# First loads in pieces beside products of ones, and pinned pairs of 64-row products, in a two-block transformer kernel

## The chip, the cores and the metric

The kernel runs on one core of one Trainium2 chip. The metric is the device time of one execution in microseconds (us), shown as the median of three runs.

## The reference

Two transformer blocks of different make run one after the other on x (512 tokens, 1024 channels); memories of 256 tokens are attended in each. Cut to what matters:

```python
def first_block(x, mem, ...):
    h = rmsnorm(x, norm_mix_g[l])
    proj = h @ w_in[l]                       # gates, conv, q, k, v of 8 heads
    y_conv = short_conv_mixer(cb, cc, cx, conv_w[l], w_conv_out[l])
    y_attn = diff_attention(q, k, v, rel_bias, lam, lam_init, subln_g[l]) @ w_attn_out[l]
    x = x + (sigmoid(gc) * y_conv + sigmoid(ga) * y_attn) @ w_mix_out[l]
    x = x + cross_attention(rmsnorm(x, norm_cross_g[l]), rmsnorm(mem, norm_mem_g[l]), ...)
    x = x + peer_ffn(rmsnorm(x, norm_ffn_g[l]), ...)      # product-key experts
    return rmsnorm(x, final_g)

def second_block(x, mem, ...):
    z = rms_norm(x, mix_norm_g[l]) @ w_in[l]
    y_nsa = nsa_mixer(...)                   # 8 heads of 64, two k/v groups
    y = concat([rms_norm(y_nsa, g_nsa), rms_norm(y_gmlp, g_gmlp), rms_norm(y_conv, g_conv)])
    x = x + y @ w_out[l]
    x = x + memory_cross_attention(x, mem, xattn_norm_g[l], ...)
    x = x + conv_ffn(x, ffn_norm_g[l], ...)
    return rms_norm(x, final_norm_g)
```

In `diff_attention` the two halves of a head, and in `nsa_mixer` two heads of different groups, have 64 channels each: their logits are products over 64 rows.

## The kernel before

The program is `mix1`, `cross`, `peer`, `mix2`, `cross` and `ffn` in sequence. Activations lie with channels on the partitions (x is a tile 128 x 8 x 512), a linear layer (`lin`, L99) sums eight blocks k of 128 channels into a bank of PSUM.

Every product is done in three (`mm3`, L83): an operand is split into hi, a cast by ScalarE, and lo, the rest, by a subtraction on VectorE (`split`, L69), and lo x hi, hi x hi and hi x lo are summed. In `lin` the first (L85, with xl) and second (L86) need w_hi, the third (L87) needs w_lo. `weights` (L73) loads w_raw on SP's queue (four buffers) and splits it: w_hi at L70, w_lo at L71 (three buffers each). The input x is scaled by a gain from the packed vectors `pk` and split by `scaled` (L109): xh on ScalarE (L111), xl on VectorE (L112). Since the normalisation's factor is one per token, the linears run on x without it; the squares of x are summed beside (`square`, sq_acc, L137 and L140), summed over channels by products with ones (`colsum`, L129), turned into rstd by small steps on VectorE (`rsqrt`, L158 to L165) and spread to all partitions by L172 (`bcast`), which ScalarE copies out as rbc (L175). What leaves the linear is multiplied with it.

`mm3s` (L89) issues the three products for two items at once: for a pair of halves A and B that lie on partitions 0 to 63 and 64 to 127, first both lo products (L93), then both hi (L95), then both last (L97). It is used in `rows` of mix1 (L311, 32 groups) and in the attention of mix2 (L1331, 32 groups), with 256, 384 or 512 columns.

Within an engine, instructions run in a fixed order. A scheduler sets it when the program is built: it goes through the program as written with a model of costs and fills an engine that would wait with what is ready, except where `keep_in_program_order` pins instructions to the order in which they are written. So an edit in one place can move rows in another. In mix2, the products of the out-projection (`out_part`, L1312, and `half_out`, L1319) serve as such fillers. At its end, eight outputs of twelve products are made from the attention's part (L1360ff); each is multiplied with rbc (ev, L1365) and added to x (L1366), and the second `cross` (L462) splits the new x, sums its squares and makes its q from the weights wq (named `ps` and `pl`), while kl and vl are splits of the keys and values read back from DRAM.

At the start `consts` (L56) loads the pack and an identity on ScalarE's queue, `body` (L1529) loads the weights of the first linear (w_in[8]) and the eight rows of x on SP's queue, and `mix1` (L184) runs two linears ahead (w_in[8], w_in[16]) before the column sum of the squares.

```python
first = pr.weights(I["w_in"][8], KT)                          # body, L1538
for k in range(KT):
    nc.sync.dma_start(out=x[:, k, :], in_=I["xT"][k * P:(k + 1) * P, :])
...
ahead = [self.lin(first, xh, xl), self.lin(w_in[16], xh, xl)] # mix1
```

## Time and profile before

| | |
|---|---|
| median of three runs | 2920.49 us (2919.88 to 2922.27) |
| profiled execution | 2924.64 us |
| its span | 2922.70 us |
| mean granted TensorE clock | 0.989 |
| TensorE busy | 2840.0 us (97%) |
| VectorE busy | 2165.6 us (74%) |
| ScalarE busy | 1234.7 us (42%) |

PE is TensorE's products and PEld its weight loads, DVE is VectorE, ACT ScalarE, POOL GpSimd, SP the engine whose queue issues most loads. In the timeline an instruction stands with its start and duration; neighbours on TensorE overlap, so the step from one start to the next is the cost of a product. What is in brackets is the time for which the engine was idle before, and what ended it. x8 means that eight records of the same kind follow each other.

### The profile page before, as it was taken

The page shows a single profiled execution, that of the slowest core. Times are in us where ns is not written, and L with a number is a line of the kernel's source. Part 1 is how long each engine was busy: PE and PEld are TensorE (multiplying, and loading weights), DVE is VectorE, ACT ScalarE, POOL GpSimd, SP SyncE. Part 2 cuts the span into 40 slices and gives each one's busy share as a digit, 9 for nine tenths or more (in the row PEclk, how much of TensorE's full clock was granted, in tenths as well). Part 3 has the DMA queues.
Part 4 walks back from the last instruction along what each step waited for, and adds up shares of the span by engine and source line. Part 5 has one row for each costly group of instructions (what it writes and reads, how often), then busy time and mean ns, then how long its engine had stood idle before and what let it go on. Part 6 is the DMA issues. An engine that isn't in the chain of part 4 may idle for free.

```text
span 2922.7 us, 40044 instructions
## 1 busy us (share of the span) xinstructions
PE 2840.0 (97%) x14683; PEld 2448.4 (84%) x14683; DVE 2165.6 (74%) x4333; ACT 1234.7 (42%) x2053; POOL 534.2 (18%) x318
## 2 busy tenths in 40 slices
PE   8999999999997899999999999999979999999998
PEld 7887888888887899999998989887857778888887
DVE  6636667566899889787787787777796768688844
ACT  3234445444333598533333333333423655433322
POOL 0000000000036201344454454431131000000000
PEclk9999999999998999999999999999989999999999
DMA  4343233542233365899999899986512004233333
GB/s 162 100 136 115 90 98 98 180 133 67 88 107 123 108 228 219 314 346 333 341 332 317 322 341 337 324 293 206 170 59 83 25 19 128 75 94 98 95 97 104
DMA packets 200496, 504.67 MB, mean 173 GB/s; under 512 B 17475, under 2 KB 88259, under 8 KB 198764
## 3 DMA queue, kind: packets, MB, share of 16 engines
q1 hardware_dynamic: 155516, 333.22, 35.2%
q0 software_dynamic: 36864, 134.23, 12.7%
q10 hardware_dynamic: 7920, 34.66, 3.0%
q8 instruction: 116, 1.90, 0.3%
q14 instruction: 80, 0.66, 0.1%
HBM read 461.46 MB, written 40.59 MB: 172 GB/s over the span
## 4 chain that ended last, share of the span: by engine, by line
PE 82%; DVE 12%; ACT 2%; DMA 2%; issue 1%; ACTq 0%; DVEq 0%
PE ps L603 14%; PE ps L85 13%; PE ps L87 13%; PE ps L86 13%; PE pl L85 2%; PE pl L86 2%; PE pl L87 2%; PE pt L87 2%; PE pt L86 2%; PE pt L85 2%; PE po L85 2%; PE po L87 1%; PE po L86 1%; DMA v_raw<-in_peer_v_dram 1%; DVE yc L1067 1%
## 5 line engine op out<-in xcount | busy, mean ns | idle before, releaser
L70 ACT CAST w_hi<-w_raw 128x1024 fp32r<-128x1024 f32 (+2 forms) x277 | 281.3, 1015 | 533.6 <-PE ps L86 411.9
L85 PE MATMUL ps<-xl,w_hi 128*128 128x512 f32 x1224 | 487.1, 398 | 12.1 <-DVE xl L112 8.2
L86 PE MATMUL ps<-xh,w_hi 128*128 128x512 f32 x1224 | 482.6, 394 | 0.0
L87 PE MATMUL ps<-xh,w_lo 128*128 128x512 f32 x1224 | 481.5, 394 | 0.2 <-DVE w_lo L71 0.2
L71 DVE TENSOR_TENSOR w_lo<-w_raw,w_hi 128x1024 fp32r<-128x1024 f32 (+2 forms) x263 | 309.1, 1176 | 98.7 <-ACT w_hi L70 93.8
L595 POOL TENSOR_TENSOR w_lo<-w_raw,w_hi 128x1024 fp32r<-128x1024 f32 x33 | 94.6, 2872 | 1063.3 <-PE pl L645 837.8
L85 PEld LDWEIGHTS ps<-xl,w_hi 128*128 128x128 f32 x1224 | 231.4, 189 | 60.8 <-DVE xl L112 8.4
L87 PEld LDWEIGHTS ps<-xh,w_lo 128*128 128x128 f32 x1224 | 231.1, 189 | 49.8 <-DVE w_lo L71 0.8
L86 PEld LDWEIGHTS ps<-xh,w_hi 128*128 128x128 f32 x1224 | 231.7, 189 | 47.6 <-issue 1.8
L860 POOL DMA_INDIRECT row<-in_peer_v_dram,eidx x128 | 196.8, 1538 | 254.5 <-DVE ya L879 204.3
L860 POOL DMA_INDIRECT row<-in_peer_u_dram,eidx x128 | 186.6, 1457 | 221.3 <-DVE dots L867 185.8
L603 PE MATMUL ps<-hfh,w_hi 128*128 128x384 f32 x1024 | 206.4, 343 | 3.3 <-ACT ring L609 1.6
L594 ACT CAST w_hi<-w_raw 128x1024 fp32r<-128x1024 f32 x128 | 134.9, 1054 | 171.7 <-PE ps L603 135.4
L603 PE MATMUL ps<-hfh,w_lo 128*128 128x384 f32 x1024 | 201.9, 338 | 3.0 <-POOL w_lo L595 3.0
L603 PE MATMUL ps<-hfl,w_hi 128*128 128x384 f32 x1024 | 201.7, 338 | 0.0
L603 PEld LDWEIGHTS ps<-hfh,w_hi 128*128 128x128 f32 x1024 | 182.8, 190 | 11.2 <-ACT w_hi L594 2.6
L603 PEld LDWEIGHTS ps<-hfh,w_lo 128*128 128x128 f32 x1024 | 179.8, 190 | 3.4 <-POOL w_lo L595 3.4
L603 PEld LDWEIGHTS ps<-hfl,w_hi 128*128 128x128 f32 x1024 | 181.7, 190 | 0.1
L595 DVE TENSOR_TENSOR w_lo<-w_raw,w_hi 128x1024 fp32r<-128x1024 f32 x95 | 116.0, 1222 | 85.8 <-ACT w_hi L594 63.4
L70 ACT CAST wh<-ring 128x384 fp32r<-128x384 f32 x103 | 52.9, 513 | 291.1 <-PE pm L86 249.7
L912 DVE TENSOR_TENSOR v_lo<-v_raw,v_hi 128x1024 fp32r<-128x1024 f32 x128 | 156.2, 1220 | 19.9 <-ACT v_hi L911 18.8
L879 DVE SCALAR_TENSOR_TENSOR ya<-row,coef,ya 128x1024 f32<-128x1024 f32 x127 | 162.8, 1282 | 0.6
(496 smaller groups left out, 6351.5 us busy)
## 6 DMA issues: line engine op xcount, KB each, us to landing
w_raw<-in_u_t_dram SPq DMA_DIRECT2D x128, 512.0 KB
v_raw<-in_peer_v_dram SPq DMA_DIRECT2D x128, 512.0 KB
w_raw<-in_w_in_dram SPq DMA_DIRECT2D x82, 512.0 KB
Gd<-gs ACTq DMA_DIRECT2D x12, 2048.0 KB
gg<-Gd SPq DMA_DIRECT2D x32, 768.0 KB
w_raw<-in_ffn_w_up_dram SPq DMA_DIRECT2D x44, 512.0 KB
w_raw<-in_ffn_w_down_dram SPq DMA_DIRECT2D x20, 512.0 KB
w_raw<-in_w_pq_dram SPq DMA_DIRECT2D x16, 512.0 KB
```

The lines of the kernel that those rows point to most:

```text
L70: self.nc.scalar.copy(out=hi, in_=src)
L71: (eng or self.nc.vector).tensor_tensor(out=lo, in0=src, in1=hi.bitcast(F32), op=ALU.subtract)
L85: mm(out, ah, bl, start=start, stop=False)
L86: mm(out, ah, bh, start=False, stop=False)
L87: mm(out, al, bh, start=False, stop=stop)
L594: i = nc.scalar.copy(out=hi, in_=raw)
L595: (nc.gpsimd if ahead else nc.vector).tensor_tensor(out=lo, in0=raw, in1=hi.bitcast(F32), op=ALU.subtract)
L603: i = nc.tensor.matmul(ps, w[:, k, :], h[:, k, :], start=p == k == 0, stop=(p, k) == (2, KT - 1))
L860: nc.gpsimd.indirect_dma_start(out=r, out_offset=None, in_=src, in_offset=bass.IndirectOffsetOnAxis(ap=eidx[:, s:s + 1], axis=0))
L879: i = nc.vector.scalar_tensor_tensor(out=ya, in0=r, scalar=coef[:, s:s + 1], in1=ya, op0=ALU.mult, op1=ALU.add)
L912: pin(tt(out=vl, in0=raw, in1=vh.bitcast(F32), op=ALU.subtract))
L1067: stt(out=o, in0=hp[:, f, k:k + S], scalar=self.col("conv_dw_w_2", 2 * k + f), in1=o, op0=ALU.mult, op1=ALU.add)
```

## The change

It has two parts.

The start: `consts` loads only the first eight columns of the pack at once, and issues nine 128x128 products of a tile of ones with itself into a bank that nobody reads. A new `first` loads the first weights in four pieces of two blocks k each, each ahead of the two rows of x that go with it, on SP's queue; the second row goes on ScalarE's queue, followed there by the rest of the pack and the identity (`consts_late`). `mix1` splits these weights piece by piece in its loop over k. One small instruction, g8, that reads the late part of the pack is pinned to its place.

The pairs: of the six products of a group in `mm3s` all but A's first are pinned to the order in which they are written.

```diff
--- before.py
+++ after.py
@@ -56,11 +56,33 @@
     def consts(self):
         nc, c = self.nc, self.const
         self.pk = c.tile([P, self.I["pack"].shape[1]], F32, name="pk")
-        nc.scalar.dma_start(out=self.pk, in_=self.I["pack"])
+        nc.scalar.dma_start(out=self.pk[:, :KT], in_=self.I["pack"][:, :KT])
         self.idt = c.tile([P, P], F32, name="idt")
-        nc.scalar.dma_start(out=self.idt, in_=self.I["idt"])
         self.ones = c.tile([P, P], F32, name="ones")
         nc.vector.memset(self.ones, 1.0)
+
+        ps = self.misc.tile([P, S], F32, name="pm")
+        for _ in range(9):
+            nc.tensor.matmul(ps[:, :P], self.ones, self.ones, start=True, stop=True)
+
+    def consts_late(self):
+        self.nc.scalar.dma_start(out=self.pk[:, KT:], in_=self.I["pack"][:, KT:])
+        self.nc.scalar.dma_start(out=self.idt, in_=self.I["idt"])
+
+    def first(self, w, x, src):
+
+        nc, wp = self.nc, self.wp
+        raw = wp.tile([P, KT, P], F32, name="w_raw", bufs=4)
+        hi = wp.tile([P, KT, P], F32R, name="w_hi")
+        lo = wp.tile([P, KT, P], F32R, name="w_lo")
+        for k in range(0, KT, 2):
+            s = slice(k, k + 2)
+            nc.sync.dma_start(out=raw[:, s, :], in_=w[:, s, :])
+            for j in (k, k + 1):
+                (nc.scalar if j == 1 else nc.sync).dma_start(out=x[:, j, :], in_=src[j * P:(j + 1) * P, :])
+            if k == 0:
+                self.consts_late()
+        return raw, hi, lo
 
     def col(self, name, j=0):
         o = PACK[name] + j
@@ -89,12 +111,13 @@
     def mm3s(self, items, start, stop):
 
         mm = self.nc.tensor.matmul
+        pin = lambda i, n: n and self.tc.keep_in_program_order(i)
+        for n, (out, ah, al, bh, bl) in enumerate(items):
+            pin(mm(out, ah, bl, start=start, stop=False), n)
         for out, ah, al, bh, bl in items:
-            mm(out, ah, bl, start=start, stop=False)
+            pin(mm(out, ah, bh, start=False, stop=False), 1)
         for out, ah, al, bh, bl in items:
-            mm(out, ah, bh, start=False, stop=False)
-        for out, ah, al, bh, bl in items:
-            mm(out, al, bh, start=False, stop=stop)
+            pin(mm(out, al, bh, start=False, stop=stop), 1)
 
     def lin(self, w, xh, xl, ps=None, m=P, eng=None):
 
@@ -194,8 +217,10 @@
         xl = mb.tile([P, KT, S], F32R, name="xl")
         w_in = I["w_in"]
         for k in range(KT):
+            if k % 2 == 0:
+                self.split(*(t[:, k:k + 2, :] for t in first))
             self.scaled(x[:, k, :], self.col("norm_mix_g", k), xh[:, k, :], xl[:, k, :])
-        ahead = [self.lin(first, xh, xl), self.lin(w_in[16], xh, xl)]
+        ahead = [self.lin(first[1:], xh, xl), self.lin(w_in[16], xh, xl)]
         acc = None
         for k in range(KT):
             acc = self.square(x[:, k, :], acc, wk, ("ex", 4))
@@ -263,7 +288,8 @@
         nc.vector.tensor_scalar(out=lm[:, 5:6], in0=lm[:, 4:5], scalar1=-0.2, scalar2=None, op0=ALU.add)
         nlam = lm[:, 5:6]
         g8 = lm[:, 6:7]
-        nc.vector.tensor_scalar(out=g8, in0=self.col("subln_g"), scalar1=1.0 - 0.2, scalar2=None, op0=ALU.mult)
+        tc.keep_in_program_order(
+            nc.vector.tensor_scalar(out=g8, in0=self.col("subln_g"), scalar1=1.0 - 0.2, scalar2=None, op0=ALU.mult))
 
 
         oth = mc.tile([P, KT, S], F32R, name="oth", tag="s0")
@@ -1535,9 +1561,7 @@
         values = [dr.tile([M, D], F32, name=f"values{n}") for n in range(2)]
         stats = {}
         x = pr.keep.tile([P, KT, S], F32, name="x")
-        first = pr.weights(I["w_in"][8], KT)
-        for k in range(KT):
-            nc.sync.dma_start(out=x[:, k, :], in_=I["xT"][k * P:(k + 1) * P, :])
+        first = pr.first(I["w_in"][8], x, I["xT"])
 
         def mem1(parts, wk):
             st = mem_prep(pr, "memT", pr.const, wk, "mem", "norm_mem_g", parts)
```

Lines after the first edits move: L85, L86, L87 of before are L107, L108, L109 of after, L70 and L71 are L92 and L93, the products of `mm3s` L93, L95, L97 are L116, L118, L120, L129 is L152, L172 is L195, L1365 and L1366 are L1391 and L1392.

The order of the instructions changes with it at these places. First TensorE in the attention of mix2, a group with 512 columns. pl_20366 and pl_20367 are the logits of the two heads A and B, kl and kh, ql and qh the splits. Before:

```order
L93 MATMUL pl_20366<-kl0_19651,qh1_19361 128x512
L95 MATMUL pl_20366<-kh0_19650,qh1_19361 128x512
L97 MATMUL pl_20366<-kh0_19650,ql1_19362 128x512
L93 MATMUL pl_20367<-kl0_19651,qh1_19361 128x512
L95 MATMUL pl_20367<-kh0_19650,qh1_19361 128x512
L97 MATMUL pl_20367<-kh0_19650,ql1_19362 128x512
L1336 MATMUL pl_20366<-Mk_19958,Id_19954 128x256
```

And after, where the two are pl_20386 and pl_20387 and po is the product of probabilities and values of an earlier group:

```order
L116 MATMUL pl_20386<-kl0_19671,qh1_19381 128x512
L107 MATMUL po_20143<-aT_19982,vh1_19935 128x256
L108 MATMUL po_20143<-aT_19982,vh1_19935 128x256
L109 MATMUL po_20143<-aT_19982,vl1_19936 128x256
L116 MATMUL pl_20387<-kl0_19671,qh1_19381 128x512
L118 MATMUL pl_20386<-kh0_19670,qh1_19381 128x512
L118 MATMUL pl_20387<-kh0_19670,qh1_19381 128x512
L120 MATMUL pl_20386<-kh0_19670,ql1_19382 128x512
L120 MATMUL pl_20387<-kh0_19670,ql1_19382 128x512
L1362 MATMUL pl_20386<-Mk_19978,Id_19974 128x256
```

A's three and then B's three have become A's first alone, other products, and five in the order B, A, B, A, B. Of the groups of mix1, before five of 256 columns have A's three and B's three apart and one of 512 has them one behind the other; after, four of the five stand as A and BABAB, one as A, B and ABAB, and the one of 512 as A and BABAB; the others stand as before. In mix2, of 16 groups of 256 columns before seven are AAA and BBB, two AAABBB, two AAB, B and AB, five ABABAB; after, nine are A and BABAB, three broken in another way, four ABABAB. Of eight groups of 384, before three are ABABAB, two A and BABAB, one AAA and BBB, one AAABBB, one AABBAB; after, four are A and BABAB and four ABABAB. Of eight groups of 512, before seven are AAABBB and one A, AA and BBB; after, all are A and BABAB.

Second, TensorE at the end of mix2, where the last output of the out-projection (pt) ends and the q products of the second cross begin. Before (w_lo_21769 is the first w_lo of wq):

```order
L87 MATMUL pt_21618<-qh2_19404,w_lo_21622 128x512
L85 MATMUL pt_21618<-ql3_19448,w_hi_21621 128x512
L86 MATMUL pt_21618<-qh3_19447,w_hi_21621 128x512
L87 MATMUL pt_21618<-qh3_19447,w_lo_21622 128x512
L85 MATMUL ps_21772<-xl_21661,w_hi_21768 128x512
L86 MATMUL ps_21772<-xh_21660,w_hi_21768 128x512
L87 MATMUL ps_21772<-xh_21660,w_lo_21769 128x512
```

After (w_lo_21789 is the first w_lo of wq, pm the column sum of cross):

```order
L108 MATMUL pt_21638<-qh3_19467,w_hi_21641 128x512
L109 MATMUL pt_21638<-qh3_19467,w_lo_21642 128x512
L107 MATMUL ps_21792<-xl_21681,w_hi_21788 128x512
L108 MATMUL ps_21792<-xh_21680,w_hi_21788 128x512
L107 MATMUL ps_21827<-xl_21681,w_hi_21823 128x512
L108 MATMUL ps_21827<-xh_21680,w_hi_21823 128x512
L107 MATMUL pl_21858<-xl_21681,w_hi_21861 128x512
L108 MATMUL pl_21858<-xh_21680,w_hi_21861 128x512
L109 MATMUL ps_21792<-xh_21680,w_lo_21789 128x512
L152 MATMUL pm_21721<-ones_82,sq_acc_21684 128x2 x4
```

The first three products of q have become six products of three outputs that need no w_lo, and then the first that does; the column sum, which stands 53 products further on before, follows at once. Of the 96 products of the out-projection's attention part, 71 stand between L172 (that of mix2's rstd) and the q products before, and 52 after it.

Third, VectorE at the same place, before:

```order
L112 SCALAR_TENSOR_TENSOR xl_21661<-x1_5092,pk_79,xh_21660 128x512
L71 TENSOR_TENSOR w_lo_21769<-w_raw_21766,w_hi_21768 128x1024
L1365 TENSOR_TENSOR ev_21615<-pl_21596,rbc_21462 128x512
L112 SCALAR_TENSOR_TENSOR xl_21661<-x1_5092,pk_79,xh_21660 128x512
L1366 TENSOR_TENSOR x1_5092<-x1_5092,ev_21615 128x512
L1365 TENSOR_TENSOR ev_21637<-pt_21618,rbc_21462 128x512
L71 TENSOR_TENSOR w_lo_21804<-w_raw_21801,w_hi_21803 128x1024
```

And after:

```order
L135 SCALAR_TENSOR_TENSOR xl_21681<-x1_5112,pk_79,xh_21680 128x512
L163 TENSOR_TENSOR sq_acc_21684<-sq_acc_21684,sq_21703 128x512
L93 TENSOR_TENSOR kl_21677<-ev_21750,kh_21676 128x512
L163 TENSOR_TENSOR sq_acc_21684<-sq_acc_21684,sq_21708 128x512
L93 TENSOR_TENSOR kl_21677<-ev_21754,kh_21676 128x512
L163 TENSOR_TENSOR sq_acc_21684<-sq_acc_21684,sq_21713 128x512
L93 TENSOR_TENSOR w_lo_21789<-w_raw_21786,w_hi_21788 128x1024
L163 TENSOR_TENSOR sq_acc_21684<-sq_acc_21684,sq_21718 128x512
```

The first w_lo of wq stood between an xl and an ev, with the ev of two outputs still to come; now it stands behind all of ev, x and xl, behind six of the seven sums of squares and two kl. From the first ev (L1391) there are 34 instructions with 512 columns ahead of it.

## Rows read from the trace of the kernel before

**Rows 1.** The page: busy time of TensorE, and 40 slices of it and its clock.
```profile
PE 2840.0 (97%) x14683; PEld 2448.4 (84%) x14683; DVE 2165.6 (74%) x4333; ACT 1234.7 (42%) x2053; POOL 534.2 (18%) x318
...
PE   8999999999997899999999999999979999999998
...
PEclk9999999999998999999999999999989999999999
```

**Rows 2.** Timeline, first 22 us: start us, us, engine line op, xcount, idle before.
```profile
1.19 5.49 SPq L1540 DMA_DIRECT2D x<-in_xT_dram  x8
...
8.24 0.79 PE L85 MATMUL ps<-xl,w_hi 128*128 128x512 f32 x1 [8.24 <-DVE xl L112]
...
9.97 2.03 ACT L111 ACTIVATE xh<-x,pk 128x512 fp32r<-128x512 f32 x3 [0.32 <-DMA x<-in_xT_dram]
...
12.95 1.03 ACT L70 CAST w_hi<-w_raw 128x1024 fp32r<-128x1024 f32 x1
...
14.01 1.23 DVE L71 TENSOR_TENSOR w_lo<-w_raw,w_hi 128x1024 fp32r<-128x1024 f32 x1 [0.25 <-ACT w_hi L70]
...
14.48 0.39 PE L85 MATMUL ps<-xl,w_hi 128*128 128x512 f32 x1
...
21.97 0.95 PE L129 MATMUL pm<-ones,sq_acc 128*128 128x2 f32 x8
```

**Rows 3.** Timeline of TensorE around five groups or parts of groups of 64-row products.
```profile
255.68 0.39 PE L93 MATMUL pl<-qk_l,qk_h 64*128 64x256 f32 x2
...
256.24 0.49 PE L85 MATMUL ps<-xl,w_hi 128*128 128x512 f32 x1
...
2276.90 0.39 PE L93 MATMUL pl<-kl,qh 64*128 64x256 f32 x1
...
2277.44 0.38 PE L1336 MATMUL pl<-Mk,Id 128*128 128x256 f32 x1
...
2283.15 0.50 PE L93 MATMUL pl<-kl,qh 64*128 64x512 f32 x1
2283.58 0.44 PE L989 MATMUL pt<-idt,ex 128*128 128x128 f32 x2
...
2299.84 0.50 PE L93 MATMUL pl<-kl,qh 64*128 64x512 f32 x1
...
2301.29 0.51 PE L1336 MATMUL pl<-Mk,Id 128*128 128x256 f32 x2
...
2352.20 0.38 PE L95 MATMUL pl<-kh,qh 64*128 64x256 f32 x1
2352.51 0.50 PE L85 MATMUL po<-aT,vh 128*128 128x512 f32 x1
```

**Rows 4.** Timeline of TensorE, end of mix2 and start of the second cross.
```profile
2409.73 1.13 PE L172 MATMUL pm<-idt,rcol 128*128 128x128 f32 x8
...
2426.82 0.39 PE L85 MATMUL ps<-xl,w_hi 128*128 128x512 f32 x1
...
2439.12 1.02 PE L129 MATMUL pm<-ones,sq_acc 128*128 128x2 f32 x8
...
2444.40 1.08 PE L172 MATMUL pm<-idt,rcol 128*128 128x128 f32 x8
```

**Rows 5.** VectorE there: its timeline, then PE, PEld, DVE, ACT, POOL busy, clock.
```profile
2411.52 0.69 DVE L1365 TENSOR_TENSOR ev<-pl,rbc 128x512 f32<-128x512 f32 x1 [0.99 <-ACT rbc L175]
...
2424.11 1.22 DVE L71 TENSOR_TENSOR w_lo<-w_raw,w_hi 128x1024 fp32r<-128x1024 f32 x1
...
2438.28 0.69 DVE L140 TENSOR_TENSOR sq_acc<-sq_acc,sq 128x512 f32<-128x512 f32 x1
...
2420.00:2430.00 10.00, 10.00 (x46) 8.27 (x45) 9.83 (x15) 6.50 (x10) 0.00 (x0) 1.00 0.40 132
```

**Rows 6.** Windows around an idle TensorE in mix2 (columns as above).
```profile
2154.30:2160.20 5.90, 0.43 (x2) 0.00 (x0) 5.90 (x7) 1.01 (x4) 3.05 (x1) 0.78 0.57 163
2160.20:2164.40 4.20, 4.16 (x11) 3.39 (x12) 4.20 (x8) 2.91 (x12) 0.00 (x0) 0.50 0.07 24
```

## The prediction

> **What bounds the kernel now.** I read the page first. TensorE is busy for 97% of the span and its granted clock stands at full in nearly every slice [rows 1]. So a change pays if it shortens TensorE's own work or one of its few waits, and a new wait of TensorE is paid in full. Then I went to the three places that the change reaches, each in the view that shows it: the timeline of the first 22 us for the loads, the timeline of TensorE around single groups of 64-row products for `mm3s`, and, since the order of the rows shows that the end of the second mix block is reshuffled, the timelines of TensorE and VectorE from 2409 to 2445 us.
>
> **Part 1, the start.** Now TensorE's first product begins at 8.24, and its first 15 products take until 14.48, 0.42 us each; the remaining 33 of the two first linears, up to L129 at 21.97, take 0.227 us each [rows 2]. These are the two levels of the clock. L129 is the column sum on which the rest of the block hangs, so the term is how much earlier the two linears end.
> The first linear can't end before the eighth row of x. ScalarE's last three xh take 2.03 from 9.97, behind a DMA [rows 2], so the third of them starts at 11.3. The bytes ahead of that row stay nearly the same; I leave it there, and with xh, an xl of like length (0.68 each) and three products the first linear ends at 13.3. The second needs its own weights: they are cast at 12.95 and their w_lo is made at 14.01 for 1.23 us [rows 2]. Of its 24 products only two come ahead of the first that reads w_lo. I estimate the cast 0.3 us earlier, since the xh ahead of it wait less; then the third product starts at 14.9, and 22 x 0.227 = 5.0 brings L129 to 19.9. **Gain 2.0 us.** It is 0 if pieces and w_lo come no earlier, and 3 if w_lo is in time and only the eighth row binds (13.3 + 24 x 0.227 = 18.7).
> The nine products of ones lie before the first real one, where TensorE does nothing for 8.24 us. A 128x128 pass costs 1.13/8 = 0.14 us (L172 in [rows 4]), double that at half clock, so nine products of two passes take at most 5 us, from about 1 to 6. Cost nothing; without that cover they would delay the first product only, and the eighth row still sets the end. The extra loads on SP and the pack's second part, read later, are hidden in the same way. The pinned g8 is one tiny instruction: nothing.
>
> **Part 2, the pairs.** All 64 groups issue six 64-row products before and after; only their order moves. A triple of one head alone with 256 columns takes 0.54 us (2276.90 to 2277.44), six in alternation take 0.56 (255.68 to 256.24), and one lone product 0.31 (2352.20 to 2352.51) [rows 3]. So two separate triples cost 1.08, and a lone A with the other five paired 0.31 + 0.56 = 0.87: 0.21 less. By the order of the rows mix1 has five groups of two triples, of which four become A and BABAB: 0.8 less. In mix2 seven groups of 256 stand as AAA and BBB: 1.5 less. Against it, one of its five fully paired groups of 256 is broken up (0.3 more). Of its 384 columns, for which I take values between those of 256 and 512, one AAA and BBB and one AAABBB get better by about 0.35 each. Of 512 columns, seven AAABBB of 1.45 us each become a lone A of 0.43 [rows 3] and a paired rest that I put at twice the lone one, 0.86; two more changes of shape, about 0.1 each, take back the rest. Mix2 gives 1.5 - 0.3 + 0.7 = 1.9, of which I take 1.5, since irregular groups remain. **Gain 2.3 us**, 0 to 4.
> These rows show that pairing pays only where both heads' products stand side by side: the lone A is paid in full. The Trainium skill, "TensorEngine Tiling (Array Packing)", section "Theoretical Speedup", promises up to 2x where the contraction has 64 rows or fewer, without a price for what is not paired; by it the lone A's would be no loss, which is rival 4.
>
> **Part 3, the hand-over to the second cross attention.** This decides. The diff doesn't show it: with the new pins the scheduler uses other fillers in the attention of mix2, and what follows is ordered anew. Let T0 be the start of L172 that spreads mix2's rstd, 2409.73 now [rows 4].
> Before: after T0 TensorE has 71 products of the out-projection, then, from 2426.82 without a break [rows 4], the q products of cross. VectorE has made the first w_lo of wq at 2424.11 + 1.2 [rows 5], ahead of its squares.
> After: 19 of the 71 stand before T0, so the q products are reached at T0 + 17.1 - 19 x 0.227 = T0 + 12.8. Six of them need no w_lo; the seventh, at T0 + 14.1, reads the first w_lo. On VectorE this w_lo now stands behind 34 instructions of 512 columns (eight each of ev, x and xl, two short w_lo, six sq_acc, two kl), which begin with the first ev at T0 + 1.79 (2411.52 [rows 5]). VectorE's pace: from 2411.52 to 2438.28 [rows 5] before has 39 instructions in 26.8 us, four of them w_lo of 1024 columns at 1.2, so (26.8 - 4.8)/35 = 0.63 for each of 512. Then 34 x 0.63 = 21.4, and 1.2 for w_lo itself, end at T0 + 24.4. **TensorE stands still for 10.3 us.** Bounds: 0.57 each (the window from 2420 to 2430: 9.83 busy, 15 instructions, two of them long [rows 5]) gives 8.3; 0.69, the duration of the ev itself, gives 12.3.
> Next late are three things. The column sum L152 stands right behind this product but needs the last sq_acc, one more VectorE instruction: **0.5 us**. From column sum to L172 it takes 5.3 us now (2439.12 to 2444.40 [rows 4]), with one long w_lo and one kl among the small steps; in after one more w_lo and a vl (1.2 + 0.6) stand in it, so 7.1, and TensorE has only the sum (0.8) and 20 products (4.5) to fill it: **1.8 us**, 0 to 2.5. And the clock: after TensorE's idle from 2154.30 to 2160.20 the granted clock was 0.50 for 4.2 us, the level of 1.2 GHz [rows 6], and half of that, 2.1 us, was lost. I expect this again or somewhat more, mostly absorbed by the 1.8 just named: **0.8 us**, 0 to 2.1.
> The 19 products change nothing in this sum: they come off the stretch after T0 and make T0 later by as much. So the loss is 10.3 + 0.5 + 1.8 + 0.8 = **13.4 us**, and what follows in cross is only shifted.
>
> **Sum.** -2.0 - 2.3 + 13.4 = +9.1 us. The profiled execution took 2924.64 (span 2922.70), so one like it would take 2933.7; the median of the runs shown is 2920.49, 4.15 lower, so I forecast **2929.6**. A change under 0.2% (5.8 us) can't be told from none here: faster means below 2914.65, slower above 2926.33.
>
> **Rivals.**
> 1. *The start pays nothing.* The loads land in the same time, and w_lo of the second linear sets L129 as before. For it: ScalarE waits for a DMA within the rows, and the second cast comes behind its other work [rows 2]. Against: the slow level of the first 15 products is what the earlier ones products and pieces take away. 2929.6 + 2.0 = 2931.6, chance 0.17.
> 2. *Everything at its good end.* VectorE runs at 0.57, the clock's loss hides, start and pairs give 3 each: 8.3 + 0.5 + 1.0 - 6 = +3.8, 2924.3, which can't be told from no change. Chance 0.13.
> 3. *No wait at the hand-over (the other side).* If VectorE were through with its 34 instructions when TensorE reaches the seventh q product, -2.0 - 2.3 = -4.3 is left, 2916.2, and with 3 for the start and 4 for the pairs 2913.5. It decides below (14.1 - 1.79 - 1.2)/34 = 0.33 us each. Against: the best pace above is 0.57, and TensorE has no other products that it could take first. For it: VectorE's instructions overlap at their ends, and the out-projection's earlier end frees PSUM sooner. Chance 0.07.
> 4. *The pairs gain in full.* If a lone product cost nothing, the lone A's of after (17 groups of 256 at 0.31, four of 384 at some 0.37, nine of 512 at 0.43) would save 10.6 more: 2919.0. Against: each lone product in [rows 3] took its time in full. Chance 0.03. This is what the rule named in part 2 of the Trainium skill would give.
> The forecast keeps 0.60, with a range of its own from 2926 to 2935.
>
> **How the numbers follow.** Slower: the forecast 0.60 and rival 1 with 0.17, 0.77. Within 0.2%: rival 2 with 0.13, rival 4 with 0.03 and of rival 3 0.03, 0.19. Faster: the other 0.04 of rival 3. The range goes from just under rival 2 to the forecast's upper end: 2923.5 to 2935.
>
> **What would show it.** In the profile of after: an idle TensorE of about 10 us near 2422, ended by VectorE's w_lo (line 93) at line 109, with a dip of the clock behind it; a wait of 1 to 2 us at L195 some 6 us later; the first real product near 6.5 at full clock, and the first block's column sum near 20 instead of 21.97; groups of `mm3s` as A, then BABAB in 0.56 (256 columns). The forecast is wrong if that idle is missing or under 8 us, which VectorE's time from the first ev to that w_lo tells; the start's term is wrong if the column sum comes after 21.

## The result, and the profile after

The change took 2938.82 us (median of six runs, 2937.38 to 2943.39), the kernel before 2920.18 (six runs, 2919.29 to 2922.27): a ratio of 1.0065, with an interval from 1.0052 to 1.0078. It is slower by 18.6 us where 9.1 were forecast, and lies above the range, which ended at 2935.

The page of after, with the lines that answer to [rows 1]:

```profile
PE 2849.4 (97%) x14701; PEld 2445.1 (83%) x14701; DVE 2166.1 (74%) x4336; ACT 1236.7 (42%) x2056; POOL 536.6 (18%) x318
...
PE   8999999999997899999999999999979998999998
...
PEclk9999999999998999999999999999989999999999
```

The span is 2941.3, 18.6 over that of before: the profiled executions, both some 4 us above their medians, differ by as much as the medians do, so the two traces may be compared row by row. In these rows nothing has moved but one slice of TensorE, the 34th, from 9 to 8, and 9.4 us more of its busy time. The timelines say where the rest lies. The table has the start of the same product in both traces:

| place (row of TensorE) | before | after | later by |
|---|---|---|---|
| column sum of the first block (L129, L152) | 21.97 | 22.88 | 0.9 |
| its rstd is spread (L172, L195) | 26.75 | 30.73 | 4.0 |
| first 64-row product of mix2's attention | 2271.70 | 2275.80 | 4.1 |
| T0, mix2's rstd is spread | 2409.73 | 2419.09 | 9.4 |
| first q product of the second cross | 2426.82 | 2431.88 | 5.1 |
| rstd of the second cross | 2444.40 | 2453.27 | 8.9 |
| rstd of ffn | 2551.38 | 2570.51 | 19.1 |

So the start lost 4.0 (a gain of 2.0 was forecast), all of mix1, cross and peer in these two traces nothing more, the groups of mix2 1.0 up to the first q product (2.3 forecast as gained by both), and from there to ffn it lost 14.1 (13.4 forecast).

**The hand-over** went as forecast in kind. This is the view of TensorE's waits in after, from 2260 to 2580 us (engine, line, what it waited for, us in total, times, longest):

```profile
PE ps L109 <- DVE w_lo L93: 9.6, 1, 9.6
PE ps L107 <- ACT w_hi L92: 0.5, 1, 0.5
PE pm L195 <- DVE rcol L188: 0.2, 1, 0.2
```

The same view of before has one wait of 0.2 us. The timeline of TensorE in after, first the seventh q product that reads the first w_lo:

```profile
2443.35 0.79 PE L109 MATMUL ps<-xh,w_lo 128*128 128x512 f32 x1 [9.62 <-DVE w_lo L93]
2444.04 1.84 PE L152 MATMUL pm<-ones,sq_acc 128*128 128x2 f32 x8
...
2446.32 0.63 PE L108 MATMUL ps<-xh,w_hi 128*128 128x512 f32 x1
2446.74 0.63 PE L109 MATMUL ps<-xh,w_lo 128*128 128x512 f32 x1
...
2453.27 1.05 PE L195 MATMUL pm<-idt,rcol 128*128 128x128 f32 x8
```

VectorE's part of it, from the first ev to the w_lo that TensorE waits for:

```profile
2420.87 0.69 DVE L1391 TENSOR_TENSOR ev<-pl,rbc 128x512 f32<-128x512 f32 x1 [1.93 <-ACT rbc L198]
...
2442.08 1.22 DVE L93 TENSOR_TENSOR w_lo<-w_raw,w_hi 128x1024 fp32r<-128x1024 f32 x1
```

And the two windows from the first q product on (us, then PE, PEld, DVE, ACT, POOL busy, granted clock, share and GB/s of the DMA engines):

```profile
2431.88:2443.35 11.47, 1.80 (x7) 0.86 (x6) 11.28 (x19) 8.09 (x14) 0.00 (x0) 0.78 0.27 87
2443.35:2451.86 8.51, 8.51 (x23) 6.79 (x24) 6.49 (x19) 2.05 (x4) 0.00 (x0) 0.50 0.76 237
```

The 34 instructions took 21.2 us (2420.87 to 2442.08), 0.62 each where 0.63 was taken, and TensorE stood still for 9.62. Then it ran for 8.51 us at a granted clock of 0.50, the level of 1.2 GHz, in which a product of 512 columns steps 0.42 us (2446.32 to 2446.74), and half of that stretch, 4.3 us, is lost: 0.8 had been put down for it. At the column sum and at L195 of cross (2453.27) no wait is left, where 0.5 and 1.8 had been put down; the 0.2 in the view is that of T0. Idle and clock make 13.9 of the 14.1.

**The start** went the other way. After has its first product at 6.73 instead of 8.24, and the next ones step 0.23 us where those of before step 0.43, the pace of the slow stretch above; by its twelfth it is 2.8 us ahead. (The view of windows gives a granted clock of 1.00 for all of the first 20 us, so the level at the start is read from the steps.) The timeline of after shows how that was lost; what answers to it is [rows 2]:

```profile
13.98 1.03 ACT L92 CAST w_hi<-w_raw 128x1024 fp32r<-128x1024 f32 x1
...
15.04 1.23 DVE L93 TENSOR_TENSOR w_lo<-w_raw,w_hi 128x1024 fp32r<-128x1024 f32 x1 [0.24 <-ACT w_hi L92]
...
16.32 0.49 PE L109 MATMUL ps<-xh,w_lo 128*128 128x512 f32 x1 [0.52 <-DVE w_lo L93]
...
21.46 0.39 PE L107 MATMUL pl<-xl,w_hi 128*128 128x512 f32 x1
...
22.88 0.47 PE L152 MATMUL pm<-ones,sq_acc 128*128 128x2 f32 x3
...
29.54 0.51 ACT L134 ACTIVATE mp<-mem,pk 128x256 fp32r<-128x256 f32 x1 [5.18 <-DMA mem<-in_memT_dram]
...
30.08 0.48 DVE L135 SCALAR_TENSOR_TENSOR mp<-mem,pk,mp 128x256 fp32r<-128x256 f32 x1 [3.28 <-ACT mp L134]
30.48 0.15 DVE L188 SCALAR_TENSOR_TENSOR rcol<-rtmp,rcol 128x4 f32<-128x4 f32 x1
...
30.73 1.13 PE L195 MATMUL pm<-idt,rcol 128*128 128x128 f32 x8 [2.62 <-issue]
```

The weights of the second linear are cast at 13.98, a us later than before, and the third product waits for their w_lo until 16.32. From there the two linears need 22 products, to 21.46, half a us earlier than before; but the column sum now stands behind six products of the next output, at 22.88. It could hardly have come earlier: VectorE's last sum of squares ends at 22.73 (22.05 and 0.68). In before it ends at 21.71, 0.26 ahead of the column sum at 21.97, so that there, too, linears that end earlier could have brought 0.3 us and no more:

```profile
21.02 0.69 DVE L140 TENSOR_TENSOR sq_acc<-sq_acc,sq 128x512 f32<-128x512 f32 x1
```

Then comes the larger loss. VectorE's last step of rstd (rcol, 30.48) stands behind the split of a row of the memory (mp, 30.08), and this behind ScalarE's mp, which waits for the load of that row until 29.54. Before, the row lands 3.0 us earlier (26.53), and the order is the other one, so that its wait costs nothing:

```profile
26.35 0.16 DVE L165 SCALAR_TENSOR_TENSOR rcol<-rtmp,rcol 128x4 f32<-128x4 f32 x1
26.53 0.51 ACT L111 ACTIVATE mp<-mem,pk 128x256 fp32r<-128x256 f32 x1 [3.16 <-DMA mem<-in_memT_dram]
...
26.75 1.05 PE L172 MATMUL pm<-idt,rcol 128*128 128x128 f32 x8
27.07 0.48 DVE L112 SCALAR_TENSOR_TENSOR mp<-mem,pk,mp 128x256 fp32r<-128x256 f32 x1 [0.56 <-ACT mp L111]
```

TensorE pays for it twice: it is idle for 2.62 us ahead of L195, and behind that the granted clock is 0.50 for 3.41 us, which costs 1.7 more:

```profile
31.83:35.24 3.41, 3.41 (x10) 2.63 (x9) 3.07 (x7) 0.59 (x1) 0.00 (x0) 0.50 0.44 149
```

The product of the linears that starts at 40.12 in before then starts at 44.23.

**The pairs.** In both traces the same 838 products run from the first 64-row product of mix2's attention up to the first q product, in after with other neighbours. Summing the steps from start to start by kind: the 192 products of 64 rows need 30.9 us instead of 34.1, as the groups were meant to, but the 240 others of 512 columns need 64.2 instead of 59.1, and all the rest 0.9 less. (About 1.0 only changes its place: where a 512-column product follows a run of 128-column ones, 22 times in after and 10 in before, the last of the run steps 0.03 us instead of 0.11 and the product behind it 0.32 instead of 0.23.) The rows show the rest, in after (the step is to the next start):

```profile
2279.96 0.40 PE L108 MATMUL ps<-nh,w_hi 128*128 128x512 f32 x1
2280.19 0.39 PE L109 MATMUL ps<-nh,w_lo 128*128 128x512 f32 x1
2280.42 0.40 PE L107 MATMUL ps<-nl,w_hi 128*128 128x512 f32 x1
2280.75 0.38 PE L116 MATMUL pl<-kl,qh 64*128 64x256 f32 x1
2281.06 0.50 PE L108 MATMUL ps<-nh,w_hi 128*128 128x512 f32 x1
2281.40 0.39 PE L109 MATMUL ps<-nh,w_lo 128*128 128x512 f32 x1
```

A 512-column product takes 0.23 (2279.96 to 2280.19), but 0.33 ahead of a lone A and 0.34 behind it, beside the 0.31 of A itself. The stretch has 58 such entries into 64-row products where before has 47; eleven more at 0.21 would be 2.3 us. Summed over all 512-column products that stand beside a 64-row one, what goes beyond 0.23 (and beyond the shift just named) is 5.3 us in after and 2.4 in before: 2.9 more. The two small waits of the view above (0.5 and 0.2, against 0.1 in before) lie in this stretch too. The Trainium skill, "TensorEngine Tiling (Array Packing)", "Key Properties", says that a change of the tiling mode drains the engine; the trace agrees in so far as it has 0.1 us more on either side; what the engine does in it can't be seen.

### The profile page after: what moved, and what is told of

It is laid out like the page before. It is cut to its first block, busy times and chain, and to the rows that moved or that the text cites. A ratio compares the mean times of both kernels' runs of the same rounds, so it can differ in the third digit from the quotient of the medians.

```text
span 2941.3 us, 40085 instructions
## 1 busy us (share of the span) xinstructions
PE 2849.4 (97%) x14701; PEld 2445.1 (83%) x14701; DVE 2166.1 (74%) x4336; ACT 1236.7 (42%) x2056; POOL 536.6 (18%) x318
## 4 chain that ended last, share of the span: by engine, by line
PE 82%; DVE 12%; ACT 2%; DMA 2%; issue 2%; ACTq 0%; DVEq 0%; SPq 0%
PE ps L629 13%; PE ps L107 13%; PE ps L109 13%; PE ps L108 13%; PE pl L107 2%; PE pl L108 2%; PE pl L109 2%; PE pt L109 2%; PE pt L108 2%; PE pt L107 2%; PE po L107 2%; PE po L108 1%; PE po L109 1%; DMA v_raw<-in_peer_v_dram 1%; DVE yc L1093 1%
## 5 line engine op out<-in xcount | busy, mean ns | idle before, releaser
L92 ACT CAST w_hi<-w_raw 128x1024 fp32r<-128x1024 f32 (+3 forms) x280 | 282.0, 1007 | 536.2 <-PE ps L108 419.9
L107 PE MATMUL ps<-xl,w_hi 128*128 128x512 f32 x1224 | 486.8, 398 | 7.1 <-DVE ev L1069 3.8
L109 PE MATMUL ps<-xh,w_lo 128*128 128x512 f32 x1224 | 481.8, 394 | 10.4 <-DVE w_lo L93 10.4
L108 PE MATMUL ps<-xh,w_hi 128*128 128x512 f32 x1224 | 482.3, 394 | 0.0
L93 DVE TENSOR_TENSOR w_lo<-w_raw,w_hi 128x1024 fp32r<-128x1024 f32 (+3 forms) x266 | 309.4, 1164 | 104.0 <-ACT w_hi L92 97.6
L109 PEld LDWEIGHTS ps<-xh,w_lo 128*128 128x128 f32 x1224 | 231.0, 189 | 60.7 <-DVE w_lo L93 11.9
L107 PEld LDWEIGHTS ps<-xl,w_hi 128*128 128x128 f32 x1224 | 231.3, 189 | 57.7 <-issue 5.1
L108 PEld LDWEIGHTS ps<-xh,w_hi 128*128 128x128 f32 x1224 | 231.4, 189 | 48.0 <-issue 1.8
L92 ACT CAST wh<-ring 128x384 fp32r<-128x384 f32 x103 | 52.9, 514 | 291.3 <-PE pm L108 251.8
```

Source lines behind the costliest of these rows:

```text
L92: self.nc.scalar.copy(out=hi, in_=src)
L93: (eng or self.nc.vector).tensor_tensor(out=lo, in0=src, in1=hi.bitcast(F32), op=ALU.subtract)
L107: mm(out, ah, bl, start=start, stop=False)
L108: mm(out, ah, bh, start=False, stop=False)
L109: mm(out, al, bh, start=False, stop=stop)
```

## The experiments

Each is timed beside runs of the kernel before on the same chip; what is given is the ratio, its interval and the medians. The diffs show the lines that matter, not the whole edit. One table of stages serves them all; the points are those of the table above, in us from the first 64-row product of mix2's attention (A) to T0, to the first q product (Q), from T0 to the rstd of cross (C), from Q to the rstd of ffn (F), and A to F. Behind F all have the same 371 us (370.8 to 371.3). Ahead of A lies the peer stage. From its own rstd (745.75 in before) to the first of mix2 (2110.06) the fourteen profiled executions take 1358.8 to 1364.7 us, in no order that the edits explain (before 1364.3, after 1364.7), so that a few us in when A comes, or between two medians, can't be put down to an edit; what lies between A and F repeats to 0.4 us in the seven versions that leave mix2 and what follows as in before, and to 1.5 in the two that have it as in after.

| | A to T0 | A to Q | T0 to C | Q to F | A to F |
|---|---|---|---|---|---|
| before | 138.0 | 155.1 | 34.7 | 124.6 | 279.7 |
| after | 143.3 | 156.1 | 34.2 | 138.6 | 294.7 |
| pairs alone | 143.3 | 156.1 | 32.7 | 137.1 | 293.2 |
| w_lo by GpSimd | 143.3 | 158.4 | 35.0 | 131.9 | 290.2 |
| three w_lo early | 143.3 | 156.1 | 34.7 | 132.8 | 288.9 |
| six pinned, w_lo early | 145.4 | 158.2 | 34.7 | 133.4 | 291.6 |
| before, w_lo early | 138.1 | 155.1 | 38.1 | 128.2 | 283.3 |
| out-products late | 143.1 | 160.8 | 36.0 | 125.4 | 286.2 |
| six pinned in mix1 | 138.1 | 155.2 | 34.7 | 124.5 | 279.6 |

**1. The start alone.** The whole change with `mm3s` as before.

```diff
-        pin = lambda i, n: n and self.tc.keep_in_program_order(i)
-            pin(mm(out, ah, bh, start=False, stop=False), 1)
+            mm(out, ah, bh, start=False, stop=False)
```

> Only the first part of the change (pack in two, first weights and rows of x in pieces, products of ones, pinned g8), with the mm3s of before. Theory A, the three parts add up and don't touch each other: the first block's rstd comes 4.0 us later than before (L195 near 30.7 instead of 26.75), since VectorE's last step of it stands behind the split of a memory row that lands only at 29.5; mix2 and the hand-over to the second cross are as before; span 2922.7 + 4 = 2926.7, median 2924.2. Rival B, the 4 us at the start are made up behind it (TensorE is only shifted against loads that have slack), or were an accident of that one execution: median 2919 to 2921. What I predicted, a gain of 2.0, would be 2918.2.

Measured: 1.0007 (0.9997 to 1.0016), 2924.61 against 2922.22. The start gains nothing, and by the interval it can't be told from before; its profile shows the same wait for the memory row, the split at 29.67, rcol at 30.08 and L194 at 30.33.

**2. The pairs alone.** The kernel before with the new `mm3s`.

```diff
-            mm(out, ah, bh, start=False, stop=False)
+            pin(mm(out, ah, bh, start=False, stop=False), 1)
```

> Only the pins in mm3s, with the start of before. Theory A: start as before (L172 at 26.75), the attention of mix2 some 1 us slower, not faster, and the wait for the first w_lo of wq of 9.6 us with the slow clock behind it, together 14 us from the first q product on: span 2937.5, median 2935. Rival B, the wait at the hand-over depends on when mix2 starts, and without the late start most of it vanishes: median under 2930. Rival C, the pairs themselves carry a loss of 4 us (the stretch up to T0 is longer by that): then T0 - start of mix2's attention is as in the whole change, while the products after T0 are not missing.

Measured: 1.0044 (1.0028 to 1.0061), 2936.04 against 2922.22, and in the table 13.5 us from A to F: nearly all of the loss is the pins' in mix2. At the end of mix1 (532.5 against 532.7) the shift against before is what it was at the start, so the pins gain nothing there either.

**3. The products of ones alone.** The kernel before with nine of them.

```diff
+        ps = self.misc.tile([P, S], F32, name="pm")
+        for _ in range(9):
+            nc.tensor.matmul(ps[:, :P], self.ones, self.ones, start=True, stop=True)
```

> The kernel before with nothing but the nine unread products of ones. Theory A, the first rstd is set by the sums of squares and the small steps on VectorE, not by the linears: the first products run at full clock (0.227 instead of 0.42 us each) and the linears end 1 to 1.5 us earlier, but L129 and L172 stay at 22.0 and 26.75; median 2920.2, no change. Rival B, the linears set it, as my prediction had it: L129 at 20.5, L172 1.5 earlier, median 2918.7.

Measured: 1.0006 (0.9996 to 1.0015), 2924.24 against 2922.22. The first products still step 0.43 us, 3.2 us after the ones:

```profile
1.06 4.21 PE L67 MATMUL pm<-ones 128*128 128x128 f32 x18 [1.06 <-DVE ones L63]
8.47 0.79 PE L89 MATMUL ps<-xl,w_hi 128*128 128x512 f32 x1 [3.21 <-DVE xl L116]
9.06 0.63 PE L90 MATMUL ps<-xh,w_hi 128*128 128x512 f32 x1
9.49 0.63 PE L91 MATMUL ps<-xh,w_lo 128*128 128x512 f32 x1
```

**4. The first two w_lo of wq by GpSimd.** The whole change; this takes them out of VectorE's queue.

```diff
+                              eng=nc.gpsimd if tag == "2" and h == 0 else None)
```

> The whole change, but the w_lo of the first two blocks of wq in the second cross are made by GpSimd instead of VectorE, so that VectorE's queue doesn't hold them back. Theory A, the wait is nothing but the place of these subtractions behind VectorE's sums: the idle of 9.6 us and the slow clock behind it go, and the median falls by 10 to 14 to 2925 to 2929. Rival B, VectorE's whole block is late after the moved products and the next thing that it makes (the third w_lo, the sums of squares) holds TensorE instead: a wait of 5 us or more stays, median above 2932.

Measured: 1.0049 (1.0033 to 1.0066), 2935.86 against 2922.22. The wait for the first w_lo is gone, but a wait of 4.1 us for a later ev takes its place, and TensorE has smaller ones on the way. This is the timeline of GpSimd and VectorE there:

```profile
2423.41 0.68 DVE L93 TENSOR_TENSOR w_lo<-w_raw,w_hi 128x512 fp32r<-128x512 f32 x1
...
2424.78 2.40 POOL L93 TENSOR_TENSOR w_lo<-w_raw,w_hi 128x1024 fp32r<-128x1024 f32 x1 [172.62 <-DVE x L1393]
2425.21 2.52 DVE L93 TENSOR_TENSOR w_lo<-w_raw,w_hi 128x512 fp32r<-128x512 f32 x1
...
2427.94 2.65 POOL L93 TENSOR_TENSOR w_lo<-w_raw,w_hi 128x1024 fp32r<-128x1024 f32 x1 [0.76 <-ACT w_hi L92]
2428.26 2.88 DVE L135 SCALAR_TENSOR_TENSOR xl<-x,pk,xh 128x512 fp32r<-128x512 f32 x1
...
2431.66 0.73 DVE L135 SCALAR_TENSOR_TENSOR xl<-x,pk,xh 128x512 fp32r<-128x512 f32 x1
```

Beside each of GpSimd's subtractions one of VectorE's took 2.5 and 2.9 us instead of 0.7, and ended 0.55 after it. So the theory that only the order of VectorE's queue costs isn't tested cleanly by this edit: it moved the work and slowed VectorE by 4.0 us.

**5. Three w_lo early, by VectorE.** The whole change with the weights of the first three q outputs made ahead of the squares; the subtractions and the sums of squares are pinned.

```diff
+        early = [self.weights(wq[n], KT, pin=True) for n in range(3)] if tag == "2" else []
+        rb, _ = self.normed(x, lambda k: self.col(g, k), xh, xl, wk, pin=tag == "2")
```

> The whole change, and besides the first three weights of wq are made ahead of the second cross's x, their three subtractions pinned on VectorE ahead of the sums of squares: by the order of the rows the first w_lo comes 21 instead of 34 instructions after the first ev, the column sum 52 instead of 7 products into q. Theory A, only the place of the w_lo matters: it is ready at T0 + 1.8 + 20 x 0.63 + 1.2 = T0 + 15.6, TensorE waits 1.5 us instead of 9.6, and the slow clock goes too: 12 less than the whole change, 2925 to 2928. Theory D, VectorE as a whole is late, since the 19 products done early were cover: what it makes next (xl of the last rows, then the q outputs' own scaling) holds TensorE instead, waits of 4 to 7 us in all stay, spread over several places: 2930 to 2934.

Measured: 1.0043 (1.0026 to 1.0060), 2933.86 against 2922.13. TensorE's waits from 2260 to 2560:

```profile
PE ps L109 <- DVE ev L526: 4.4, 1, 4.4
PE ps L111 <- DVE w_lo L93: 1.5, 1, 1.5
```

The wait for w_lo falls to 1.5 as expected. But what was taken off VectorE at that place comes due later: the q outputs wait 4.4 us until VectorE can evict them. From A to F it still takes 9.2 us more than before. The time from T0 to the rstd of cross, which is VectorE's, is 34.7, as in before (34.2 in after, 32.7 to 38.1 over all runs), and from the first ev on VectorE is busy for 31.5 of 33.0 us, as for 31.6 of 32.9 in before. So this stretch looks bound by VectorE's sum of work, whatever order it is done in.

**6. Early w_lo in the kernel before.** The same edit without the change.

> The kernel before with only the three early w_lo of the second cross (71 products of the out-projection still stand after L172). Theory A and D alike: VectorE makes the w_lo in time behind 71 products' cover (first one at T0 + 18.5 against T0 + 17.1 + 6 x 0.23 = T0 + 18.5): nothing, or a wait under 2 us; 2920 to 2923. Were the early weights themselves a loss (their buffers of w_hi and w_lo are held longer) it would show here: over 2925.

Measured: 1.0009 (0.9999 to 1.0018), 2925.28 against 2922.13; 3.6 us more from A to F, with T0 to C 3.4 longer (TensorE waits 1.4 for a w_lo, and the clock falls behind it). In the kernel before, the scheduler's own order is better than the early one. The edit has a price of its own, so 5 understates what the order costs: of the 9.2 that stay there, some 3.6 can be this.

**7. The out-products held behind T0.** The whole change; the first product of each later output and L172's pin the order, so that 74 of the 96 products stand behind T0, as 71 do before.

```diff
-            ps = out_part(n, pool, tag, I["w_out_2"][:, :, :4, :], qs)
+            ps = out_part(n, pool, tag, I["w_out_2"][:, :, :4, :], qs, n >= 1)
```

> The whole change, but the first product of each output of mix2's out-projection from the second on is pinned behind L195 of mix2's rstd, so that 74 instead of 52 of its 96 products stand after T0 (71 before the change); the scheduler then puts the first w_lo of wq 21 instructions after the first ev again, and the column sum 53 products into q. Theory D, from T0 to the second rstd VectorE's chain takes 34.7 us in all versions, and the 19 products that were pulled ahead of T0 were its cover: the first q product to the ffn's rstd takes 124.6 again instead of 138.6, 13 to 14 us less than the whole change, 2925 to 2927. Rival, the wait comes from the pinned groups (ScalarE and VectorE behind at the end of the attention): 7 us or more of the 14 stay, 2932 or more.

Measured: 1.0031 (1.0020 to 1.0043), 2930.21 against 2921.65: half of the loss is back. Behind T0, TensorE waits only 0.8 us, at the column sum of cross (for sq_acc). The other waits of this view lie ahead of T0, where after had 0.7:

```profile
PE pm L154 <- DVE ql L1331: 2.1, 1, 2.1
PE pl L107 <- ACT ex L1004: 0.9, 1, 0.9
PE pl L118 <- ACT ex L1004: 0.8, 1, 0.8
PE pm L154 <- DVE sq_acc L165: 0.8, 1, 0.8
PE pm L107 <- DVE aT L93: 0.3, 1, 0.3
```

This is the run that divides the 15.0 us from A to F. With the cover behind T0 restored 8.5 are gone (294.7 to 286.2), and 6.5 stay. The 6.5 are accounted for. T0 comes 143.1 after A, although no extra product stands ahead of it (three fewer do): TensorE waits 4.1 us for the chain of the attention instead of doing out-products, 4.0 more than in before, and behind the last of these waits the granted clock falls, which costs 1.7; the 0.8 at the column sum is the rest.

```profile
2409.84:2413.26 3.42, 3.42 (x9) 2.63 (x8) 2.63 (x14) 0.62 (x1) 0.00 (x0) 0.50 0.08 7
```

That the attention itself ends later stands in the traces of before and after, too. This is the last sum of squares of its output; it starts 132.2 after A in before and 136.6 in after (136.2 in this run):

```profile
2403.86 0.69 DVE L140 TENSOR_TENSOR sq_acc<-sq_acc,sq 128x512 f32<-128x512 f32 x1 [4.97 <-ACT sq L137]
...
2412.43 0.69 DVE L163 TENSOR_TENSOR sq_acc<-sq_acc,sq 128x512 f32<-128x512 f32 x1 [6.12 <-ACT sq L160]
```

So with the pinned groups the attention ends some 4 us later, with the 19 products ahead of T0 or without them, and these had only filled that.

**8. The start with VectorE's order set right.** The start alone, with rstd's last steps and the third and fourth memory split pinned, so that rstd goes first.

```diff
-            stt(out=r, in0=w, scalar=1.5, in1=r, op0=ALU.add, op1=ALU.mult)
+            i = stt(out=r, in0=w, scalar=1.5, in1=r, op0=ALU.add, op1=ALU.mult)
+            if pin:
+                self.tc.keep_in_program_order(i)
```

> Only the start of the change (mm3s of before), with the last steps of the first block's rstd pinned ahead of the third and fourth split of the memory on VectorE. Theory A, the late rstd is the split's wait for its DMA: L195 comes 4.8 us after L152 as before, near 27.3, the wait of 2.6 us and the slow clock behind it go, and the start costs 0.5 instead of 2.4 to 4: equal to before (0.0 to +0.6). Rival B, the late loads (the second weights are cast 1 us later) hold the sums of squares and the rest: L152 later than 22.9 or L195 near 30 all the same, +2 to +3 stay.

Measured: 1.0003 (0.9993 to 1.0012), 2923.06 against 2922.13. In the timeline rcol no longer waits for the load:

```profile
26.10 0.16 DVE L189 SCALAR_TENSOR_TENSOR rcol<-rtmp,rcol 128x4 f32<-128x4 f32 x1
26.99 1.05 PE L198 MATMUL pm<-idt,rcol 128*128 128x128 f32 x8
28.19 0.51 ACT L133 ACTIVATE mp<-mem,pk 128x256 fp32r<-128x256 f32 x1 [4.57 <-DMA mem<-in_memT_dram]
```

The product that starts at 40.12 in before starts at 39.03 here, 1.1 ahead, where after has it 4.1 behind. So in the traces the order was the loss, though the row lands late here too. The times of this run and of run 1 (1.0003 and 1.0007) are too near to each other to show it, and against before the start gains next to nothing.

**9. The same without the products of ones.**

> The run with the start alone and rstd's steps pinned, without the nine products of ones. Theory: the ones bring nothing that lasts, since the second linear waits for its w_lo near 15.5 and the column sum for the last sum of squares near 22 whatever the first linear does: the first products at 0.43 instead of 0.23 us each, L153 at 22.1 and L198 at 27.0 as with them, time within 0.5 us of that run. Rival: without them the clock rises late, the two linears end 1 to 2 us later than with them and the gain of 1.2 at 29 us is gone.

Measured: 1.0000 (0.9991 to 1.0009), 2920.01 against 2920.14. Its first products (from 6.53) step 0.43 us, its rstd is spread at 28.29, and the product of 40.12 is 0.2 behind before: the 1.1 of run 8 are gone, as its rival had it. But the second weights also landed later, their cast waited for them until 14.61 (13.22 in run 8), and in run 12 it came at 14.72 with the ones. So the trace doesn't separate the two. The time is no other than with the ones, but a gain of 1.1 us lies within the interval.

**10. All six products pinned, three w_lo early.** The start of before; A's first product is pinned too, which was to bring ABABAB together. The diff is against the `mm3s` of after.

```diff
-            pin(mm(out, ah, bl, start=start, stop=False), n)
+            pin(mm(out, ah, bl, start=start, stop=False), 1)
```

> The start of before; mm3s with all six products of a group pinned (also A's first), and the three early w_lo of the second cross as in the run above. By the order, of mix1's groups all of 384 and 512 columns and 11 of 256 are six in alternation, of mix2's 12 of 256; the other 20 are A and BABAB. Theory A: 2 to 3 us less in the groups of both blocks than with the pins of the change, and no long wait at the hand-over: 2918 to 2921 beside 2920 of before. Theory D: 2924 to 2929, the waits at the hand-over outweigh the groups. Rival C, the groups cost by their entries (a lone A has two changes of shape): mix2's attention not shorter than before.

Measured: 1.0055 (1.0039 to 1.0072), 2937.51 against 2922.13, above what theories A and D had; rival C's sign, an attention that isn't shorter, is there (A to T0). In mix2 this is worse than the change with the same early w_lo: A to Q takes 2.1 more. There TensorE waits for the attention's chain; six of these waits, 2.4 us in all, are for an exponential at the first product of a half group (L96, ended by ex). Mix1, by contrast, ended earlier than before.

**11. All six pinned in mix1 alone.** The kernel before with this one edit.

```diff
-                       for pl, r in zip(pls, (slice(0, 64), slice(64, 128)))], True, True)
+                       for pl, r in zip(pls, (slice(0, 64), slice(64, 128)))], True, True, True)
```

> The kernel before with all six products of a group pinned in mix1 alone. Theory: 2.7 us less at the end of mix1 (522 us), 13 of them kept by the end only if TensorE bounds the peer stage as well; ratio 0.9991. Rival: swallowed, ratio 1.0000.

Measured: 0.9992 (0.9983 to 1.0001), 2917.49 against 2920.14. The same product behind mix1's attention starts at 522.04 before (L85) and here, 0.4 behind at the column sum, at

```profile
519.62 0.48 PE L85 MATMUL ps<-xl,w_hi 128*128 128x512 f32 x1
```

so mix1 is 2.4 us shorter, or 2.8 from its column sum on. It has the lowest median of all versions; by its interval it just can't be told from before.

**12. Both together:** the start of 8 and the six of 11.

> The start of the change with the last steps of rstd pinned ahead of the memory's third split, and all six products of a group pinned in mix1 alone; mix2 and the hand-over in the order of before. Theory: the start gives 1.2 and the groups of mix1 2.7 (what the traces of the two runs above showed at 29 us and at 522 us), nothing is late behind them: 4 less than before, ratio 0.9987, 2916 beside 2920. Rival: the peer stage, whose end hangs on gathers and not on TensorE, swallows it: ratio 0.9995 to 1.0005.

Measured: 0.9999 (0.9990 to 1.0008), 2921.08 against 2920.14. No gain in the times, as the rival had it. In this execution the second weights came late again, the column sum at 23.62, so that the start lost 0.4; mix1 gained what it did in 11, and cross has its rstd at 633.62, 2.5 ahead of before (636.16). Whether the peer stage swallows that can't be told, since its own spread is larger.

## Why the prediction was wrong

The sign was right, and the size about half. By terms:

- **Start, forecast -2.0, measured +4.0. This step failed, at three places.** "I estimate the cast 0.3 us earlier": it came 1.0 later. "L129 is the column sum on which the rest of the block hangs, so the term is how much earlier the two linears end": the sum needs VectorE's last sum of squares as well, which ends at 21.71 in before and at 22.73 in after, so the linears had 0.3 us to give and not 2.0. And the part that costs most, from 26.75 to 30.73, was not looked at: the text follows the change to the column sum and says of what is read later that it is "hidden in the same way". Between the sum and L172 VectorE's order had changed, and put a load that had been harmless, and now lands 3.0 later, ahead of rstd; TensorE's wait for it is 2.62 us and the slow clock behind it 1.7. Run 8 shows in its trace that the wait goes when, against run 1, only that order is turned round. Rival 1 ("the start pays nothing") came nearest: run 8 measured its size, and the loads are its reason, but it hung L129 on w_lo and not on the squares, and had no added wait. Of the 4.0 some is the execution's own: run 1 as timed allows -0.9 to +4.7.
- **Products of ones, cost nothing:** right as far as the times tell (runs 3 and 9), and no gain from them shows either.
- **Pairs in mix1, forecast -0.8, measured about 0; in mix2, forecast -1.5, measured +1.0. This step failed.** The prices of a triple, of six in alternation and of a lone A were right, and the 64-row products themselves got 3.2 us shorter. What was mis-sized is the border: two "changes of shape, about 0.1 each" were counted for seven groups of 512 columns alone, where the trace has eleven more entries and 2.9 us of borders more, besides 0.5 of new waits. -3.2 + 2.9 + 0.5 is +0.2, so that 0.8 us of the measured +1.0 have no place in my reading. Rival 4 fell with the same rows: a lone product is paid in full, and its borders too. That contradicts what rival 4 made of the Trainium skill, "TensorEngine Tiling (Array Packing)", "Theoretical Speedup", and not the section itself: its "Up to 2×" is an upper limit and says nothing of a product that stands alone.
- **Hand-over, forecast +13.4, measured +14.1: right in its mechanism**, with the wait at the line, on the engine and for the tile that were named. The idle was 9.6 (10.3), the pace 0.62 (0.63). That the sum came out right to 0.7 is in part luck, since terms were off that nearly cancel: the clock cost 4.3 (0.8), the slow stretch having lasted 8.5 us and not 4.2 as in [rows 6], after an idle 1.6 times as long; and in that stretch VectorE caught up, so that the waits at the column sum and at L195 are gone (none instead of 0.5 and 1.8), where I had let the wait absorb the clock. Rival 3 fell: 0.62 a piece is far from the 0.33 that it needed.
- **"The 19 products change nothing in this sum"** holds for the sum up to the q products but hid a cause. I took them for a free choice of the scheduler. They fill a gap: with the pinned groups the attention ends some 4 us later, in after and in run 7 alike. With them back behind T0, 8.5 of the 15.0 are gone, and the gap shows as waits of TensorE, with the clock behind them.
- **The sum by the times.** The start alone is 2.4 us and the pairs alone 13.8 over before, 16.2 of the 18.6; the intervals, 2.8 us and 4.8 us each way, leave room for the rest.

Why the pinned groups end later I can only argue: A's second product now stands behind B's first and so behind the bank that B needs, which lets A's exponential start later. Run 7 has two waits for banks that ScalarE's exponentials (ex) free, one of them at a group's first product, and run 10, with A's first product pinned as well, has six at first products, 2.4 us in all, which fits; no run separates it. Run 7 also moved other rows, so that its pins may have a part in its waits.

## What to carry to other kernels

An order that is pinned at one place is paid where the scheduler rearranges the rest: compare the order of every engine over the whole program, at the start as well as at the end, and look for a load that has come to stand ahead of a chain's last step. Products that wait as fillers are a store of cover; where VectorE is the slower engine behind the next join, using them up ahead of the join turns them into a standstill, and the standstill costs the clock on top. Ask of a term at a join what else the join waits for: here the column sum needed the squares as much as the linears. For half-height products count the borders between tile heights and not only the products: a lone one pays two.

## What was not expected of the hardware

GpSimd and VectorE did not work side by side on subtractions from SBUF: beside 2.40 and 2.65 us of GpSimd, VectorE's 128x512 took 2.52 and 2.88 instead of 0.68 and 0.73, each ending 0.55 after GpSimd's. The Trainium skill, "SBUF — State Buffer", section "SBUF: two separate sides", says that the two share a pair of ports that one of them holds for a whole instruction, also against a VectorE operation with two inputs from SBUF; the trace agrees.

And the same products of ones did not always bring the full pace. Eight profiled executions have them. In after and in runs 5, 8 and 12 the first real products behind them step 0.23 us, in run 5 only for the first few; in runs 1, 3, 4 and 7 they step 0.43, as in before. How long the ones took doesn't tell the two kinds apart: 3.90 us in after and 3.88 in run 5, but 4.21 in the other six.
